# First tokens' output rows through VectorE block transpositions, a trip through DRAM and GpSimd, in place of TensorE transpositions

## The chip, the cores and the metric

The kernel runs on one core of a Trainium2 chip. The core has a matrix engine (TensorE, PE in the profile; its weight loads are PEld), three engines for elementwise work (VectorE = DVE, ScalarE = ACT, GpSimd = POOL), an engine that mostly issues transfers (SyncE = SP), and 16 DMA engines that all queues share. Each engine works through its own list of instructions in order and waits on semaphores. SBUF is the on-chip memory of 128 partitions, PSUM the accumulator memory that TensorE writes. The metric is the device time of one execution in microseconds (us).

## The reference: what is computed

One decoder layer on two groups of tokens that share the weights: 256 prompt tokens and 8 x 8 sample tokens, 320 tokens in all, with a model width of 2048. After the attention and convolution branches, the part that matters here is

```
h  = x + merged @ w_o
hn = rms_norm(h, g_ffn)
h  = h + (silu(hn @ w_gate) * (hn @ w_up)) @ w_down      # inner width 5632
y  = rms_norm(h, g_final)                                # h * rsqrt(mean(h*h) + 1e-6) * g_final
```

The final norm needs, for each token, the sum of squares over all 2048 features before any output of that token can be scaled.

## The kernel before, in words

Everything is kept with features on partitions: `hT` (its tile is called `xv` in the profile) holds 16 chunks of 128 features x 320 tokens. The weights are streamed from HBM in 512 KB pieces (`wraw`); ACT rounds each to the fast matmul format (`whi`, L129) and DVE forms the remainder (`wlo`, L130), so that three products, high by high, high by low and low by high, give the precision. TensorE runs these products back to back.

The last product, with `w_down`, is made in blocks of 512 output features (`down(half, c0)`), in two halves of the inner width (28 and 16 chunks). The last block of the second half (features 1536 to 2047, `E0` = 1536) is written out apart as the final loop (L1120 on), with its split weights held in spare tiles so that the same weights can be used twice. Each block has one `set` per pair of inner chunks (i = 0 to 6; the last set has two pairs), and its results are added to `hT` by DVE (`first`: the first 128 tokens; `rest`: the other 192).

The first 128 tokens leave in rows, a token per partition (`y0`, in tile `ya`), the other 192 with features on partitions. For the rows a part of the product (low rows of the activation by high weights, `dl`) is already made in row form and kept in `ylow`, 512 columns for each of the first three blocks; for the last block all of the correction is made in rows in the PSUM tile `rowacc`. For the first three blocks, `rows_of(c0)` transposes four 128 x 128 blocks of `hT` on TensorE against an identity matrix (L1058, PSUM tile `fa`), adds `ylow` on DVE (L1060), takes the sum of squares on ACT into one column of `ssf` (`row_squares`, L1050) and multiplies by `g_final` on DVE (L1062). `rest_of` does the squares and the scaling for the other 192 tokens; their squares are added up in `yacc`.

These steps are put off: they stand in a list, `pending`, and are taken from it at fixed places of the next block, once in the sets and once after the evictions. A context `after(...)` makes an instruction follow another in the same engine's list, without a semaphore; everything else of the order is set by a scheduler that ranks ready instructions by their place in the program and its own cost estimates. The result is one fixed list for each engine.

At the end come, on DVE, the three small instructions that sum three columns of `ssf` (`s3`, `h3`, L1138 to L1140), the evictions of the last block (L1146, L1147, L1153, L1158) with the additions to `yacc` (L1151, L1154); on TensorE eight row products (L1165), the sum of `yacc` over partitions (`pn`, L1169), the last four transpositions into `rowacc` (L1172) and the other 24 row products; then the scale factors and the stores. Tile `jk` has one buffer, `wraw` four, `whi` and `wlo` three.

Of the kernel before, what the change touches and what calls it, by code (L numbers as in the profile page):

```python
# [8 lines left out]
F32 = mybir.dt.float32  # L9
# [43 lines left out]
def hybrid_layer(ctx: ExitStack, tc: tile.TileContext, a: dict, o: list):  # L53
# [18 lines left out]
    def ps_aux(name):  # L72
        return aux[0].tile([P, 512], F32, tag="aux", name=name)
# [3 lines left out]
    def u(s):  # L77
        uid[0] += 1
        return f"{s}_{uid[0]}"
# [867 lines left out]
    def down(half, c0):  # L947

        nf, f0 = FH[half], half * FH[0]
        ps = [ps_acc(u("dn")) for _ in range(4)]  # L950
        low = ps_aux(u("dl")) if c0 < E0 else rowacc
        sets = [[k] for k in range(0, nf, 2)]
        sets[-2:] = [sets[-2] + sets[-1]]
        for i, k0s in enumerate(sets):
            parts = {}
            for k0 in k0s:
                raw = wp.tile([P, 2, 512], F32, tag="wraw", name=u("wraw"), bufs=4)
                nc.sync.dma_start(raw, w_d[c0 // 512, :, f0 + k0:f0 + k0 + 2, :])
                hi, lo = down_parts()
                split_to(hi, lo, raw)  # L960
                for j in range(2):
                    parts[k0 + j] = (hi[:, j, :], lo[:, j, :])
            end = i == len(sets) - 1
            order = [(k, c) for k in parts for c in range(4)]
            if end or i == 0:
                order.sort(key=lambda kc: kc[1])
            for k, c, m in in_turn(order, 2 if end else 4):
                cs = slice(c * P, (c + 1) * P)
                if m == 0:
                    nc.tensor.matmul(  # L970
                        turns(placed(ps[c])), parts[k][0][:, cs], turns(a_move(k)), start=k == 0, stop=False
                    )
                elif m == 1 and c == (2 if k > k0s[0] + 1 else 0):
                    nc.tensor.matmul(  # L974
                        low, a_low(k), parts[k][0], start=k == 0, stop=k == nf - 1 and c0 < E0
                    )
                elif m == 2:
                    last["mm"] = nc.tensor.matmul(  # L978
                        turns(placed(ps[c])[:, :, 0:JT]), parts[k][1][:, cs], turns(a_move(k)[:, :, 0:JT]),
                        start=False, stop=k == nf - 1,  # L980
                    )
            if len(pending) > 1 and i == 3:
                with after(last["lo"], last["mm"]):
                    pending.pop()()
        mark["out"] = []
        for c in range(4):
            k = c0 // P + c
            got, (first, rest) = placed(ps[c]), h_parts(k)
            nc.vector.tensor_add(first, first, got[:, :, 0:JR])
            nc.vector.tensor_add(rest, rest, got[:, :, JR:JT])  # L990
            mark["out"].append(nc.vector.tensor_add(rest, rest, got[:, :, JT:]))
        if c0 < E0:
            ys = ylow[:, c0:c0 + 512]
            if half == 0:
                nc.scalar.activation(ys, low, AF.Copy)
            else:
                nc.vector.tensor_add(ys, low, ys)
        if pending:
            with after(mark["out"][-1]):
                pending.pop()()  # L1000

    for half in range(2):
        f0 = 0 if half == 0 else FH[0]
# [37 lines left out]
        if half == 1:  # L1041
# [6 lines left out]
            def row_squares(i, src):  # L1048
# [2 lines left out]
                    jk[:, :src.shape[-1]], src, AF.Square, scale=D ** -0.5, accum_out=ssf[:, i:i + 1]  # L1051
                )

            def rows_of(c0):

                pt = ps_aux(u("fa"))
                for c in range(4):
                    nc.tensor.transpose(pt[:, c * P:(c + 1) * P], hT[:, c0 // P + c, 0:P], ident)  # L1058
                y = y0[:, c0:c0 + 512]
                nc.vector.tensor_add(y, pt, ylow[:, c0:c0 + 512])  # L1060
# [26 lines left out]
        for c0 in range(0, D if half == 0 else E0, 512):  # L1087
            down(half, c0)
            if half == 1:
                pending.append(lambda c0=c0: rows_of(c0))  # L1090
                pending.append(lambda c0=c0: rest_of(range(c0 // P, c0 // P + 4)))


    nf = FH[1]
# [22 lines left out]
    for i, ks in enumerate(sets):  # L1117
# [20 lines left out]
    nc.vector.tensor_reduce(s3, ssf[:, 0:3], axis=AX.X, op=ALU.add)  # L1138
    nc.vector.tensor_scalar(s3, s3, EPS, None, op0=ALU.add)
    nc.vector.tensor_scalar(h3, s3, -0.5, None, op0=ALU.mult)  # L1140
    sqs = []
    for c in range(4):
        k = E0 // P + c
# [14 lines left out]
        nc.vector.tensor_add(first, first, placed(ps[c])[:, :, 0:JR])  # L1158
    for c in range(4):
        rest_factor(E0 // P + c)  # L1160

    for k in range(nf):
        (wh, wl), xhk, xlk = held[k], a_first(k), a_low(k)
# [111 lines left out]
```

## Time and profile before

| what | value |
|---|---|
| runs of the kernel before | 1601.37, 1600.56 and 1600.24 us, median 1600.56 us |
| span of the profiled execution, first to last instruction | 1598.6 us (1.96 us less than the median; no time of its own is given for the profiled one) |
| PE busy | 1590.2 us, 99% of the span |
| PEld, DVE, ACT, POOL busy | 1554.8, 884.0, 650.6, 78.3 us |
| granted TensorE clock, mean | 0.998 |
| last load of weights issued | about 1566 us from the span's start |
| last matmul ends | about 1591 us |

Times below are counted from the span's start. A row of the timeline gives start, duration, engine, line, operation, output and inputs, and, in brackets, how long the engine had been idle and what ended it. "xN" means N like instructions merged; their duration is then that of the whole group. Matmuls overlap in the pipeline, so what one occupies is read from the start of one to the start of the next. Idle time on an engine other than TensorE costs nothing unless TensorE, or the end, waits for it.

### The profile page before, as it was taken

The page shows a single profiled execution, that of the slowest core. Times are in us where ns is not written, and L with a number is a line of the kernel's source. Part 1 is how long each engine was busy: PE and PEld are TensorE (multiplying, and loading weights), DVE is VectorE, ACT ScalarE, POOL GpSimd, SP SyncE. Part 2 cuts the span into 40 slices and gives each one's busy share as a digit, 9 for nine tenths or more (in the row PEclk, how much of TensorE's full clock was granted, in tenths as well). Part 3 has the DMA queues.
Part 4 walks back from the last instruction along what each step waited for, and adds up shares of the span by engine and source line. Part 5 has one row for each costly group of instructions (what it writes and reads, how often), then busy time and mean ns, then how long its engine had stood idle before and what let it go on. Part 6 is the DMA issues. An engine that isn't in the chain of part 4 may idle for free.

```text
span 1598.6 us, 26406 instructions
## 1 busy us (share of the span) xinstructions
PE 1590.2 (99%) x10957; PEld 1554.8 (97%) x10957; DVE 884.0 (55%) x1315; ACT 650.6 (41%) x928; POOL 78.3 (5%) x123
## 2 busy tenths in 40 slices
PE   9999999999999999999999999999999999999998
PEld 9999999999999999999999999998888999999887
DVE  7879565445555545556555555553444455555556
ACT  7555433433333334444333333333333334444443
POOL 1101311000000003320000000000000000000000
PEclk9999999999999999999999999999999999999999
DMA  7554546545444444444445454455555445545552
GB/s 271 178 169 138 185 145 195 169 156 156 157 157 158 158 158 158 156 154 155 157 159 159 158 158 156 154 155 162 156 157 158 157 158 158 158 156 154 184 180 93
DMA packets 74399, 258.13 MB, mean 161 GB/s; under 512 B 8552, under 2 KB 11928, under 8 KB 74152
## 3 DMA queue, kind: packets, MB, share of 16 engines
q1 hardware_dynamic: 71880, 249.86, 49.4%
q0 software_dynamic: 1968, 5.90, 1.3%
q8 instruction: 86, 1.41, 0.4%
q10 hardware_dynamic: 432, 0.69, 0.1%
q14 instruction: 33, 0.27, 0.0%
HBM read 253.30 MB, written 5.08 MB: 162 GB/s over the span
## 4 chain that ended last, share of the span: by engine, by line
PE 99%; DVE 0%; ACT 0%; DVEq 0%; issue 0%
PE fu L186 18%; PE fg L186 18%; PE dn L970 9%; PE ga L186 7%; PE wo L186 7%; PE gc L186 7%; PE dn L978 6%; PE B L186 3%; PE C L186 3%; PE H L186 3%; PE q L186 3%; PE ya L186 3%; PE yc L186 3%; PE dl L974 2%; PE kv L376 2%; PE dn L1125 1%
## 5 line engine op out<-in xcount | busy, mean ns | idle before, releaser
L130 DVE TENSOR_TENSOR wlo<-wraw,whi 128x1024 fp32r<-128x1024 f32 (+1 forms) x460 | 561.7, 1222 | 585.4 <-ACT whi L129 470.0
L129 ACT ACTIVATE whi<-wraw 128x1024 fp32r<-128x1024 f32 (+1 forms) x460 | 485.5, 1056 | 720.4 <-PE fu L186 129.4
L186 PE MATMUL fu<-hh_t,whi 128*128 128x320 f32 x704 | 205.1, 301 | 0.0
L186 PE MATMUL fu<-hl_t,whi 128*128 128x320 f32 x704 | 205.1, 301 | 0.0
L186 PE MATMUL fg<-hl_t,whi 128*128 128x320 f32 x704 | 205.1, 301 | 0.0
L186 PE MATMUL fg<-hh_t,whi 128*128 128x320 f32 x704 | 205.1, 301 | 0.0
L186 PE MATMUL fu<-hh_t,wlo 128*128 128x320 f32 x704 | 158.9, 301 | 0.0
L186 PE MATMUL fg<-hh_t,wlo 128*128 128x320 f32 x704 | 158.9, 301 | 0.0
L970 PE MATMUL dn<-a_t,whi 128*128 128x512 f32 x640 | 155.4, 382 | 0.0
L186 PEld LDWEIGHTS fu<-hh_t,whi 128*128 128x128 f32 x704 | 131.8, 187 | 0.0
L186 PEld LDWEIGHTS fg<-hh_t,whi 128*128 128x128 f32 x704 | 131.8, 187 | 0.0
L186 PEld LDWEIGHTS fu<-hl_t,whi 128*128 128x128 f32 x704 | 131.8, 187 | 0.0
L186 PEld LDWEIGHTS fg<-hl_t,whi 128*128 128x128 f32 x704 | 131.8, 187 | 0.0
L970 PEld LDWEIGHTS dn<-a_t,whi 128*128 128x128 f32 x640 | 115.5, 187 | 16.3 <-issue 0.9
L186 PEld LDWEIGHTS fu<-hh_t,wlo 128*128 128x128 f32 x704 | 116.2, 187 | 0.0
L186 PEld LDWEIGHTS fg<-hh_t,wlo 128*128 128x128 f32 x704 | 116.2, 187 | 0.0
L978 PEld LDWEIGHTS dn<-a_t,wlo 128*128 128x128 f32 x640 | 97.7, 188 | 6.9
L978 PE MATMUL dn<-a_t,wlo 128*128 128x320 f32 x640 | 103.4, 301 | 0.0
L186 PE MATMUL wo<-m_l,whi 128*128 128x320 f32 x256 | 74.6, 301 | 0.0
L186 PE MATMUL ga<-xl_t,whi 128*128 128x320 f32 x256 | 74.6, 301 | 0.0
L186 PE MATMUL gc<-xl_t,whi 128*128 128x320 f32 x256 | 74.6, 301 | 0.0
L186 PE MATMUL wo<-m_h,whi 128*128 128x320 f32 x256 | 74.6, 301 | 0.0
(312 smaller groups left out, 2659.0 us busy)
## 6 DMA issues: line engine op xcount, KB each, us to landing
wraw<-in_w_in_dram SPq DMA_DIRECT2D x128, 512.0 KB, 3.8
wraw<-in_w_gate_dram SPq DMA_DIRECT2D x88, 512.0 KB, 3.7
wraw<-in_w_up_dram SPq DMA_DIRECT2D x88, 512.0 KB, 3.7
wraw<-in_w_down_dram SPq DMA_DIRECT2D x88, 512.0 KB, 3.7
wraw<-in_w_o_dram SPq DMA_DIRECT2D x32, 512.0 KB, 3.8
wraw<-in_w_conv_out_dram SPq DMA_DIRECT2D x16, 512.0 KB, 3.7
wraw<-in_w_attn_out_dram SPq DMA_DIRECT2D x16, 512.0 KB, 3.6
wraw<-in_w_kv_dram SPq DMA_DIRECT2D x6, 512.0 KB, 7.5
```

Source lines behind the costliest of these rows:

```text
L129: last["hi"] = nc.scalar.activation(hi, src, AF.Copy)
L130: last["lo"] = nc.vector.tensor_sub(lo, src, hi.bitcast(F32))
L186: last["mm"] = nc.tensor.matmul(turns(fives(ps[c][:, :T])), w[:, k, c * P:(c + 1) * P], turns(x(kc)), start=(kc == 0 and i == 0), stop=(kc ...
L376: last["mm"] = nc.tensor.matmul(turns(fives(ps[c][:, :T])), w[:, k, c * P:(c + 1) * P], turns(x(kc)), start=(kc == 0 and m == 0), stop=(kc ...
L970: nc.tensor.matmul(turns(placed(ps[c])), parts[k][0][:, cs], turns(a_move(k)), start=k == 0, stop=False)
L974: nc.tensor.matmul(low, a_low(k), parts[k][0], start=k == 0, stop=k == nf - 1 and c0 < E0)
L978: last["mm"] = nc.tensor.matmul(turns(placed(ps[c])[:, :, 0:JT]), parts[k][1][:, cs], turns(a_move(k)[:, :, 0:JT]), start=False, stop=k == ...
L1125: nc.tensor.matmul(turns(placed(ps[c])[:, :, JR:]), held[k][0][:, cs], turns(a_move(k)[:, :, JR:]), start=k == 0, stop=k == nf - 1,)
```

## The change

For the first three blocks the 12 transpositions on TensorE, the three DVE additions of `ylow` and the three DVE multiplications by `g_final` are gone. In their place, for each block:

- `rows_turned(c0)`: one DVE instruction transposes 32 x 32 blocks in place of 128 x 128 (`STREAM_TRANSPOSE`, 128 x 512, into a tile with the tag `jk`); `blocks_out` then stores it to DRAM (`scr`, 256 KB) and loads it back in four pieces of 32 partitions (64 KB each), all from the GpSimd queue, which puts the 32 x 32 blocks in their places. The columns of a block stand in another order in `y0` then; `ylow` is kept in that order, `g_final` is given so and the output is put back in order outside of the measured time.
- `rows_of(c0)`: GpSimd adds `ylow` and multiplies by `g_final`; ACT takes the squares as before.

Three pieces are put on `pending` per block in place of two, and they are taken in sets 1 and 3 and after the evictions: `rows_turned`, `rest_of`, `rows_of`, first in, first out. The three small sums `s3`, `h3` are written behind the last evictions in the program.

```diff
+    def blocks_out(dst, src):
+        scr = dr.tile([P, 4, dst.shape[2]], F32, tag=f"scr{dst.shape[2]}", name=u("scr"), bufs=2)
+        nc.gpsimd.dma_start(scr, src)
+        for b in range(4):
+            nc.gpsimd.dma_start(dst[32 * b:32 * b + 32], scr[:, b].rearrange("(a i) m -> i a m", a=4))
...
-            if len(pending) > 1 and i == 3:
+            if pending and i in (1, 3):
                 with after(last["lo"], last["mm"]):
-                    pending.pop()()
+                    pending.pop(0)()
...
-            ys = ylow[:, c0:c0 + 512]
+            ys = ylow[:, c0:c0 + 512].rearrange("p (a c f) -> p c a f", a=4, c=4)
+            got = low.rearrange("p (c a f) -> p c a f", a=4, c=4)
...
+            def rows_turned(c0):
+                x = op.tile([P, 512], F32, tag="jk", name=u("jk")).rearrange("p (b m) -> p b m", b=4)
+                nc.vector.transpose(
+                    x.rearrange("p b (c f) -> p c b f", c=4),
+                    hT[:, c0 // P:c0 // P + 4, 0:P].rearrange("p c (b t) -> p c b t", b=4),
+                )
+                blocks_out(y0[:, c0:c0 + 512].rearrange("p (a m) -> p a m", a=4), x)
+
             def rows_of(c0):
-                pt = ps_aux(u("fa"))
-                for c in range(4):
-                    nc.tensor.transpose(pt[:, c * P:(c + 1) * P], hT[:, c0 // P + c, 0:P], ident)
                 y = y0[:, c0:c0 + 512]
-                nc.vector.tensor_add(y, pt, ylow[:, c0:c0 + 512])
+                nc.gpsimd.tensor_tensor(y, y, ylow[:, c0:c0 + 512], op=ALU.add)
                 row_squares(c0 // 512, y)
-                nc.vector.tensor_mul(y, y, gfb[:, c0:c0 + 512])
+                nc.gpsimd.tensor_tensor(y, y, gfb[:, c0:c0 + 512], op=ALU.mult)
...
-                pending.append(lambda c0=c0: rows_of(c0))
+                pending.append(lambda c0=c0: rows_turned(c0))
                 pending.append(lambda c0=c0: rest_of(range(c0 // P, c0 // P + 4)))
+                pending.append(lambda c0=c0: rows_of(c0))
...
-    s3, h3, v, s, r = (op.tile([P, 1], F32, name=n) for n in ("s3", "h3", "vf", "sf", "rr"))
-    nc.vector.tensor_reduce(s3, ssf[:, 0:3], axis=AX.X, op=ALU.add)
-    nc.vector.tensor_scalar(s3, s3, EPS, None, op0=ALU.add)
-    nc.vector.tensor_scalar(h3, s3, -0.5, None, op0=ALU.mult)
...                                      # the four lines stand after the last evictions
```

How the fixed lists move is seen at three places. The first is ACT at the second block's row squares (`jk,ssf<-ya`); `a_t` and `whi` are the rounded weights of the last blocks. Before:

```order
L129 ACTIVATE whi_15420<-wraw_15418 128x1024
L129 ACTIVATE a_t_12679<-wraw_15513 128x1024
L129 ACTIVATE whi_15444<-wraw_15442 128x1024
L129 ACTIVATE a_t_12679<-wraw_15517 128x1024
L129 ACTIVATE whi_15450<-wraw_15448 128x1024
```

With the change:

```order
L129 ACTIVATE whi_15431<-wraw_15429 128x1024
L1058 ACTIVATE jk_15515,ssf<-ya 128x512
L129 ACTIVATE a_t_12679<-wraw_15519 128x1024
L129 ACTIVATE whi_15455<-wraw_15453 128x1024
L129 ACTIVATE a_t_12679<-wraw_15523 128x1024
L129 ACTIVATE whi_15461<-wraw_15459 128x1024
```

The second block's squares, which need the trip through DRAM and GpSimd's addition, now stand ahead of five roundings of weights.

The second place is ACT at the end, the squares of the third block and of the last block's four chunks (`sq_15718` to `sq_15734` before, `sq_15719` to `sq_15735` after). Before:

```order
L129 ACTIVATE whi_15547<-wraw_15545 128x1024
L1050 ACTIVATE jk_15593,ssf<-ya 128x512
L1066 ACTIVATE sq_15636<-xv 128x192
L1066 ACTIVATE sq_15640<-xv 128x192
L1071 ACTIVATE xv<-xv 128x192 x2
L1066 ACTIVATE sq_15718<-xv 128x192
L1071 ACTIVATE xv<-xv 128x192
L1066 ACTIVATE sq_15723<-xv 128x192
```

With the change:

```order
L1080 ACTIVATE sq_15645<-xv 128x192
L1085 ACTIVATE xv<-xv 128x192 x2
L1080 ACTIVATE sq_15719<-xv 128x192
L1085 ACTIVATE xv<-xv 128x192
L1058 ACTIVATE jk_15682,ssf<-ya 128x512
L1080 ACTIVATE sq_15724<-xv 128x192
L1085 ACTIVATE xv<-xv 128x192
L1080 ACTIVATE sq_15730<-xv 128x192
L1085 ACTIVATE xv<-xv 128x192
L1080 ACTIVATE sq_15735<-xv 128x192
```

The third block's row squares have moved behind the first chunk's square of the last block and stand ahead of the other three.

The third place is DVE at the end (`dn_15557` to `dn_15560` are the last block's four accumulators). With the change, from the last split on:

```order
L130 TENSOR_TENSOR wlo_15554<-wraw_15551,whi_15553 128x1024
L1065 STREAM_TRANSPOSE jk_15593<-xv 128x4x4x32
L1092 TENSOR_TENSOR yacc<-yacc,sq_15633 128x192
L1092 TENSOR_TENSOR yacc<-yacc,sq_15637 128x192
L1092 TENSOR_TENSOR yacc<-yacc,sq_15641 128x192
```

and some rows further:

```order
L1158 TENSOR_TENSOR xv<-xv,dn_15558 128x192
L1162 TENSOR_TENSOR yacc<-yacc,sq_15719 128x192
L1164 TENSOR_TENSOR xv<-xv,dn_15558 128x128
L1173 TENSOR_REDUCE s_15745<-ssf 128x1
L1157 TENSOR_TENSOR xv<-xv,dn_15559 128x192
L1174 TENSOR_SCALAR s_15745<-s_15745 128x1
L1158 TENSOR_TENSOR xv<-xv,dn_15559 128x192
L1162 TENSOR_TENSOR yacc<-yacc,sq_15724 128x192
```

Before, the reduction (L1138) stood ahead of all the last block's evictions; now it stands between those of the second and the third chunk, and the third block's transposition stands behind the last split of weights. On GpSimd, which has nothing else in this stretch, each block has five transfers, then the addition, then the multiplication:

```order
L222 DMA scr_15595<-jk_15593 128x512
L224 DMA ya<-scr_15595 32x4x128 x4
L1074 TENSOR_TENSOR ya<-ya,ylow 128x512
L1076 TENSOR_TENSOR ya<-ya 128x512
L1285 UNCONDITIONAL_BRANCH
```

These rows are the third block's; nothing stands ahead of its transfers but the second block's multiplication.

More of the change, by code (lines that the diff above doesn't have):

```diff
@@ L1160, in hybrid_layer @@
         rest_factor(E0 // P + c)
+    s3, h3, v, s, r = (op.tile([P, 1], F32, name=n) for n in ("s3", "h3", "vf", "sf", "rr"))
+    nc.vector.tensor_reduce(s3, ssf[:, 0:3], axis=AX.X, op=ALU.add)
+    nc.vector.tensor_scalar(s3, s3, EPS, None, op0=ALU.add)
+    nc.vector.tensor_scalar(h3, s3, -0.5, None, op0=ALU.mult)
     for k in range(nf):
@@ L1255 @@
         inputs[n] = by_block(_np.asarray(inputs[n])[0])
+    last = E0 // 512
+    g = _np.asarray(inputs["g_final"])
+    turned = g[:E0].reshape(last, 4, 4, 32).transpose(0, 2, 1, 3)
+    inputs["g_final"] = _np.concatenate([turned.reshape(-1), g[E0:]])
     inputs["w_down"] = by_block(_np.asarray(inputs["w_down"])[0], 512)
@@ L1270 @@
     ncv = _np.asarray(res.pop()).transpose(2, 1, 0)
+    y0 = _np.asarray(res[0])
+    turned = y0[:, :E0].reshape(P, last, 4, 4, 32).transpose(0, 1, 3, 2, 4)
+    res[0] = _np.concatenate([turned.reshape(P, E0), y0[:, E0:]], axis=1)
     rest = _np.asarray(res[1]).transpose(2, 1, 0).reshape(T - P, D)
```

8 lines of the change are left out of this document (4 added, 4 removed).

## The prediction

> **What bounds the kernel now.** I read the page's busy times and its chain first, then the timeline of each engine over the last 65 us, then the transfers of the GpSimd queue.
>
> ```profile
> PE 1590.2 (99%) x10957; PEld 1554.8 (97%) x10957; DVE 884.0 (55%) x1315; ACT 650.6 (41%) x928; POOL 78.3 (5%) x123
> PE 99%; DVE 0%; ACT 0%; DVEq 0%; issue 0%
> ```
>
> TensorE is the bound from start to end: the chain that ended last is 99% PE. So an instruction taken off PE is worth what it occupies there, and work put on the other engines costs nothing until PE, or the last store, waits for it. These are the PE rows that the change touches, and the end:
>
> ```profile
> 1534.76 0.60 PE L1058 MATMUL fa<-ident,xv 128*128 128x128 f32 x4
> 1535.11 1.61 PE L970 MATMUL dn<-a_t,whi 128*128 128x512 f32 x6
> ...
> 1555.29 1.93 PE L970 MATMUL dn<-a_t,whi 128*128 128x512 f32 x8
> ...
> 1561.96 0.60 PE L1058 MATMUL fa<-ident,xv 128*128 128x128 f32 x4
> 1562.32 1.26 PE L1125 MATMUL dn<-a_t 128*128 128x384 f32 x6
> ...
> 1567.40 0.60 PE L1058 MATMUL fa<-ident,xv 128*128 128x128 f32 x4
> 1567.75 1.58 PE L1125 MATMUL dn<-a_t 128*128 128x384 f32 x8
> ...
> 1582.69 2.03 PE L1165 MATMUL rowacc<-a_t 128*128 128x512 f32 x8
> 1584.56 0.51 PE L1169 MATMUL pn<-yacc,ones_r 128*128 128x192 f32 x2
> ```
>
> Each group of transpositions occupies 0.35, 0.36 and 0.35 us from its start to the next. The last two rows are the only place where PE needs something late from DVE: `pn` reads `yacc`. DVE there:
>
> ```profile
> 1536.83 0.35 DVE L991 TENSOR_TENSOR xv<-xv,dn 128x192 f32<-128x192 f32 x1
> ...
> 1564.30 0.69 DVE L1060 TENSOR_TENSOR ya<-fa,ylow 128x512 f32<-128x512 f32 x1
> 1564.90 1.22 DVE L130 TENSOR_TENSOR more<-wraw,more 128x1024 fp32r<-128x1024 f32 x1
> ...
> 1573.04 0.68 DVE L1060 TENSOR_TENSOR ya<-fa,ylow 128x512 f32<-128x512 f32 x1
> ...
> 1575.46 0.15 DVE L1138 TENSOR_REDUCE s<-ssf 128x1 f32<-128x3 f32 x1
> 1575.64 0.36 DVE L1078 TENSOR_TENSOR yacc<-yacc,sq 128x192 f32<-128x192 f32 x1
> ...
> 1581.66 0.35 DVE L1146 TENSOR_TENSOR xv<-xv,dn 128x192 f32<-128x192 f32 x1
> ...
> 1584.06 0.36 DVE L1154 TENSOR_TENSOR yacc<-yacc,sq 128x192 f32<-128x192 f32 x1
> ```
>
> The third chunk's evictions start at 1581.66 and the last addition to `yacc` ends at 1584.42, 0.14 us before `pn`. PE does not wait there now, but there is no slack: what delays DVE at 1581.66 delays PE by nearly as much.
>
> **The sum: gain.** PE loses 0.35 + 0.36 + 0.35 = 1.06 us of work. By the end all PE times stand 1.06 us earlier, so the third chunk's evictions are due at 1581.66 - 1.06 = 1580.60.
>
> **First two blocks.** ACT has the second block's row squares ahead of five roundings; the rows of before there, and of the third block's squares:
>
> ```profile
> 1544.35 1.06 ACT L129 ACTIVATE whi<-wraw 128x1024 fp32r<-128x1024 f32 x1 [1.08 <-PE dl L974]
> 1547.81 1.06 ACT L129 ACTIVATE a_t<-wraw 128x1024 fp32r<-128x1024 f32 x1 [2.40 <-DMA wraw<-in_w_down_dram]
> 1548.77 1.05 ACT L129 ACTIVATE whi<-wraw 128x1024 fp32r<-128x1024 f32 x1
> ...
> 1570.81 1.06 ACT L129 ACTIVATE whi<-wraw 128x1024 fp32r<-128x1024 f32 x1 [1.53 <-DMA wraw<-in_w_down_dram]
> 1573.82 0.63 ACT L1050 ACTIVATE jk<-ya 128x512 f32<-128x512 f32 x1 [1.95 <-DVE ya L1060]
> 1574.36 0.19 ACT L1050 ACTIVATION_READ_ACCUMULATOR jk<-ya 128x1 f32 x1
> ```
>
> The `whi` of 1548.77 feeds the PE set at 1555.29. One `a_t` rounding (0.96 to the next start) and its own 1.06 stand ahead of that set, so ACT may be held until 1553.2. The second transposition stands behind the eviction of 1536.83, at 1537.1: its chain may take 16.1 us. Below I put the chain at 11.0 us in a quiet machine and 16.1 at worst, so I cost this at nothing; ACT's lead over PE is the cover, and beyond it PE would wait for what is over. I take the first block the same way, its chain being the same. `rest_of` stays in set 3 of the next block. The evictions of `ylow` with four-dimensional shapes I take at their old price, DVE having idle time ahead of them.
>
> **Third block.** Its transposition stands on DVE behind the last split, where the addition of `ylow` stood at 1573.04. One removed addition (0.60, from 1564.30 to 1564.90) frees the buffer of the last load that much earlier; the `whi` of 1570.81 waits for that load, so 0.60 comes off, and 0.71 of earlier PE: it starts at 1573.04 - 0.60 - 0.71 = 1571.73. From there everything is one chain: transposition, store, four loads, GpSimd's addition, ACT's square, DVE's reduction. The rows nearest to its links:
>
> ```profile
> out_dram<-ya SPq DMA_DIRECT2D x2, 256.0 KB, 2.8
> out_dram<-vn POOLq DMA_DIRECT2D x1, 128.0 KB, 4.0
> bias_s<-e_scr POOLq DMA_DIRECT2D x1, 68.0 KB, 2.9
> e_scr<-e_sb POOLq DMA_DIRECT2D x1, 24.0 KB, 2.2
> cv<-in_cache_v_dram POOLq DMA_DIRECT2D x8, 128.0 KB, 5.0
> ...
> 40.31 0.52 POOL L459 DMA_DIRECT2D e_scr<-e_sb  x1 [23.21 <-PE prb L211]
> 42.76 0.54 POOL L460 DMA_DIRECT2D bias_s<-e_scr  x1 [1.43 <-DMA e_scr<-e_sb]
> ...
> 608.53 0.72 POOL L909 TENSOR_TENSOR sq<-xv 128x320 f32<-128x320 f32 x1 [0.87 <-DVE xv L899]
> 622.10 1.70 POOL L909 TENSOR_TENSOR sq<-xv 128x320 f32<-128x320 f32 x1
> ...
> 1574.00:1582.00 8.00, 8.00 (x54) 8.00 (x53) 4.39 (x15) 3.35 (x10) 0.00 (x0) 1.00 0.00 0
> ```
>
> The last row (its last two figures are the DMA share and GB/s) says that the DMA engines are idle from 1574 to 1582, so I take prices near the quiet rows:
>
> - Transposition: no row shows one. I take the DVE row of equal size, 0.69; as upper end 1.22, the row of twice as many elements.
> - Store of 256 KB from GpSimd's queue: between 2.2 (24 KB, same queue) and 4.0 (128 KB, same queue, beside weight loads). SP's 256 KB store at a quiet end takes 2.8; I take 3.1.
> - Four loads of 64 KB: three issues of 0.54 ahead of the last, 1.62, and its landing. The nearest row is 68 KB, 2.9, which I take: 4.5. Ends: 2.2 and 5.0, so 3.8 and 6.6.
> - GpSimd's addition: 0.72 for 320 columns, times 512/320, 1.15. The same operation took 1.70 where DVE worked beside it; upper end 2.72.
> - ACT's square with its read of the sum: 1573.82 to 1574.55, 0.73.
> - Hand-overs: from landing to the dependent GpSimd issue 42.76 - 40.31 - 2.2 = 0.25, twice; three between engines at 0.10 (1573.72 to 1573.82): 0.8.
>
> Sum: 0.69 + 3.1 + 4.5 + 1.15 + 0.73 + 0.8 = 10.97 (11.0). By the low ends 0.69 + 2.2 + 3.8 + 1.15 + 0.73 + 0.8 = 9.4, by the high ends 1.22 + 4.0 + 6.6 + 2.72 + 0.73 + 0.8 = 16.1. The reduction can start at 1571.73 + 10.97 = 1582.70 and takes 0.18 to the next start (1575.46 to 1575.64). The evictions behind it, due at 1580.60, start at 1582.88: 2.28 late. The two other small sums, which now stand between dependent evictions, add about 0.1. ACT's remaining squares, queued behind the row squares, come in time for evictions so late. So PE waits 2.4 us ahead of `pn`, and everything behind it (24 row products, scales, stores) follows.
>
> The Trainium skill, "DMA: Bandwidth & Descriptors", section "Anatomy of one DMA — SWDGE (gpsimd) path", states some 2.0 us plus bytes/436e3 for such a transfer. My estimate from it is 2.6 for the store and 2.15 for a load, 1.25 us less in the sum, and the end would be unchanged within 0.1 us instead of 1.3 later, within the band of the forecast below. The row of 128 KB at 4.0 speaks against it under load, that of 24 KB at 2.2 for it.
>
> A second rule there speaks against the change: "GPSIMD Engine Reference", section "Engine selection", gives two-input elementwise work to VectorE, GpSimd being about twice as slow, and the page's key points name contention with VectorE instructions of two SBUF inputs. The trace agrees (0.72 against 1.70 above). By the page's factor alone the addition would take 1.4, the sum 0.2 more.
>
> **Sum.** -1.06 + 2.4 = +1.3 us: the span of 1598.6 becomes 1599.9. The runs' median lies 1.96 above the span, so 1601.9 us. That is inside 0.2% (3.2 us), about what a measurement of this kernel can tell from no change.
>
> **Rivals.**
>
> *The chain is hidden* (15 in 100). If the chain takes under 8.7 us (1580.60 - 0.18 - 1571.73), only the small sums in DVE's list remain: 0.18 + 0.1. Then -1.06 + 0.3 = -0.8, 1599.8 us. For it: idle DMA engines and the row of 2.2. Against it: even the low ends give 9.4.
>
> *The trip through DRAM runs at its loaded prices* (30 in 100), the slower side. One mechanism: a GpSimd transfer takes 4 to 5 us whatever else runs, as in the rows of 4.0 and 5.0. At 4.0 and 6.6, with the rest as above, the chain is 14.0 and the wait 5.4: +4.3, 1604.9 us. With the other high ends too, 16.1, it is 1607.0. The rise is past 0.2% from a chain of 12.9 us on. For it: most GpSimd rows of before are so long. Against it: all those were taken beside weight loads, and the window of 1574 is empty.
>
> *The second block starves PE* (3 in 100): a chain above 16.1 us at 1537.1 holds ACT beyond 1553.2. One us over is one us of PE, on top of the third block's wait; some 1608. Only the far ends together reach it.
>
> The forecast has 50 in 100, for waits from 0.7 to 4.2 us; 2 in 100 are left for a gain above 3.2 us, for which no row gives a place.
>
> **How the numbers follow.** Low end 1599.6: the hidden chain, 0.2 lower for the spread of runs. High end 1606.0: the loaded prices with about half of their spread. Outside lie some 5 in 100 below and 13 above. Faster by over 0.2% 0.03; slower 0.32, from the loaded prices and the starved second block; the same 0.65.
>
> **What would show it.** No `fa` rows on PE and three starts 0.35 earlier. A gap on PE ahead of `pn` of some 2.4 us, ended by DVE's `yacc`; on DVE an idle time ahead of the reduction, ended by ACT's `jk`; on ACT, `jk` waiting for GpSimd's `ya` with idle time in front. The store's and loads' times to landing decide between the rivals. No idle time on PE in the blocks at 1528 to 1562. The prediction would be wrong if a block transposition takes many times 0.69, if GpSimd's transfers land slower than 5 us in a quiet machine, or if GpSimd's work slows DVE's evictions at the end.

## The result, and the profile after

| what | before | after |
|---|---|---|
| median of the runs, us | 1600.51 (1599.53 to 1601.37, and one of 4330.16) | 1602.87 (1601.82 to 1604.79) |
| ratio, with its 95% interval | | 1.0016 (1.0010 to 1.0022) |
| profiled execution: time, span, us | span 1598.6 | 1604.61, span 1602.9 |
| PE busy, us | 1590.2 | 1591.4 |

The changed kernel is 0.16% (2.4 us) slower: inside the band of 0.2% (its interval reaches just beyond it), and 1.0 us above the time forecast. The profiled execution is one of the slower ones of the changed kernel. The other executions lie in two groups, about two thirds of them from 1601.8 to 1603.5 and the rest from 1604.0 to 1604.8; why there are two is part of what follows.

The busy times and the chain on the page of the kernel after:

```profile
PE 1591.4 (99%) x10945; PEld 1554.9 (97%) x10945; DVE 882.5 (55%) x1312; ACT 650.0 (41%) x928; POOL 94.5 (6%) x144
PE 98%; DVE 1%; DMA 1%; ACT 0%; POOL 0%; issue 0%; DVEq 0%; ACTq 0%
```

PE has 12 matmuls fewer and yet 1.2 us more of busy time. Its timeline, from a place ahead of the change to its end:

```profile
1496.88 0.62 PE L981 MATMUL dl<-whi,a_t 128*128 128x512 f32 x2
...
1535.31 1.58 PE L977 MATMUL dn<-a_t,whi 128*128 128x512 f32 x6
...
1582.12 2.01 PE L1180 MATMUL rowacc<-a_t 128*128 128x512 f32 x8
1585.98 0.59 PE L1184 MATMUL pn<-yacc,ones_r 128*128 128x192 f32 x2 [1.85 <-DVE yacc L1165]
1586.41 0.60 PE L1187 MATMUL rowacc<-ident,xv 128*128 128x128 f32 x4
1586.76 1.66 PE L1180 MATMUL rowacc<-a_t 128*128 128x512 f32 x4
1588.22 3.12 PE L1180 MATMUL rowacc<-more,a_t 128*128 128x512 f32 x8
1591.18 2.92 PE L1180 MATMUL rowacc<-whi,a_t 128*128 128x512 f32 x12
```

The first row stands at 1496.33 in the trace of before, so this execution is 0.55 us late before anything has changed; in the other traces of this document the same row stands between 1495.84 and 1496.78, whatever the kernel, so such offsets are taken off before two traces are compared. The transpositions `fa` are gone from PE. Ahead of `pn` PE now waits for `yacc`, 1.85 us. And eight row products that took 2.0 us take 3.12. The windows over that stretch say why (PEclk is the third figure from the end):

```profile
1584.00:1586.00 2.00, 0.15 (x2) 0.02 (x1) 1.92 (x8) 1.22 (x3) 0.07 (x1) 1.00 0.00 0
1586.00:1588.00 2.00, 2.00 (x10) 1.75 (x11) 0.94 (x1) 0.75 (x3) 0.00 (x0) 0.81 0.03 8
1588.00:1590.00 2.00, 2.00 (x6) 1.54 (x6) 1.79 (x5) 0.00 (x0) 0.00 (x0) 0.50 0.00 0
1590.00:1592.00 2.00, 2.00 (x9) 1.66 (x8) 2.00 (x5) 0.00 (x0) 0.00 (x0) 0.84 0.34 132
```

Behind the wait the granted clock falls to 0.50 and is back after 3.4 us (1587.2 to 1590.6, worked out from the clocks of the three windows). The last matmul ends at 1594.10. In the trace of before the last row of PE is this:

```profile
1588.11 2.92 PE L1165 MATMUL rowacc<-whi,a_t 128*128 128x512 f32 x12
```

From the start of `pn` to the end of the last matmul it is 1594.10 - 1585.98 = 8.12 us after, 1591.03 - 1584.56 = 6.47 before: 1.65 us more, 1.5 of them from the fall (an execution without a fall, the next run, takes 6.62).

The chain of the third block, on the timelines of DVE, POOL and ACT (and one of the last evictions):

```profile
1573.11 0.70 DVE L1065 STREAM_TRANSPOSE jk<-xv 128x512 f32<-128x512 f32 x1
...
1582.73 0.16 DVE L1173 TENSOR_REDUCE s<-ssf 128x1 f32<-128x3 f32 x1 [1.74 <-ACT jk L1058]
...
1583.45 0.83 DVE L1162 TENSOR_TENSOR yacc<-yacc,sq 128x192 f32<-128x192 f32 x1
```

```profile
1538.64 0.60 POOL L222 DMA_DIRECT2D scr<-jk  x1 [10.69 <-DVE jk L1065]
1543.54 2.18 POOL L224 DMA_DIRECT2D ya<-scr  x4 [4.29 <-DMA scr<-jk]
1549.95 1.28 POOL L1074 TENSOR_TENSOR ya<-ya,ylow 128x512 f32<-128x512 f32 x1 [4.23 <-DMA ya<-scr]
...
1574.11 0.60 POOL L222 DMA_DIRECT2D scr<-jk  x1 [20.76 <-DVE yacc L1092]
1576.70 2.18 POOL L224 DMA_DIRECT2D ya<-scr  x4 [1.99 <-DMA scr<-jk]
1580.53 1.41 POOL L1074 TENSOR_TENSOR ya<-ya,ylow 128x512 f32<-128x512 f32 x1 [1.65 <-DMA ya<-scr]
1582.77 1.30 POOL L1076 TENSOR_TENSOR ya<-ya 128x512 f32<-128x512 f32 x1 [0.84 <-ACT jk L1058]
```

```profile
1551.26 0.63 ACT L1058 ACTIVATE jk<-ya 128x512 f32<-128x512 f32 x1 [5.70 <-POOL ya L1074]
...
1552.84 1.05 ACT L129 ACTIVATE whi<-wraw 128x1024 fp32r<-128x1024 f32 x1
...
1554.73 1.05 ACT L129 ACTIVATE whi<-wraw 128x1024 fp32r<-128x1024 f32 x1
...
1570.87 1.06 ACT L129 ACTIVATE whi<-wraw 128x1024 fp32r<-128x1024 f32 x1 [1.62 <-DMA wraw<-in_w_down_dram]
...
1581.97 0.63 ACT L1058 ACTIVATE jk<-ya 128x512 f32<-128x512 f32 x1 [1.82 <-POOL ya L1074]
```

From the transposition to the reduction it is 1582.73 - 1573.11 = 9.62 us in the third block. In the second block, with weight loads on the same DMA engines, the trip takes far longer: from the store's issue to the first load's it is 4.90 us (1538.64 to 1543.54) where the third block has 2.59, and behind the loads' issues POOL is idle for 4.23 us where it has 1.65.

The last stores take nearly as long as before (2.9, 3.0 and 1.8 us to landing against 2.8, 2.8 and 1.9, medians of one to two stores), but the stretch from the last matmul to the end of the span has grown from 1598.6 - 1591.03 = 7.6 to 1602.9 - 1594.10 = 8.8 us. The waits of SyncE's queue over that stretch, after and then before, show part of it (us in all, times, longest; L1285 and L1266 are the program's end):

```profile
SPq L1285 <- DMA out_dram<-ya: 2.8, 2, 2.0
...
SPq L1285 <- PEq L1285: 1.1, 2, 0.9
```

```profile
SPq L1266 <- DMA out_dram<-ya: 2.6, 2, 1.8
SPq L1266 <- PEq L1266: 0.7, 2, 0.5
```

So for the profiled execution: 0.55 of offset, -1.06 of transpositions, 0.1 in the second block, 1.85 of wait, 1.65 behind the wait and 1.2 at the end make 4.3 us, which is the difference of the spans, 1602.9 - 1598.6.

### The profile page after: what moved, and what is told of

It is laid out like the page before. It is cut to its first block, busy times and chain, and to the rows that moved or that the text cites. A ratio compares the mean times of both kernels' runs of the same rounds, so it can differ in the third digit from the quotient of the medians.

```text
span 1602.9 us, 26432 instructions
## 1 busy us (share of the span) xinstructions
PE 1591.4 (99%) x10945; PEld 1554.9 (97%) x10945; DVE 882.5 (55%) x1312; ACT 650.0 (41%) x928; POOL 94.5 (6%) x144
## 3 DMA queue, kind: packets, MB, share of 16 engines
q8 instruction: 86, 1.41, 0.3%
## 4 chain that ended last, share of the span: by engine, by line
PE 98%; DVE 1%; DMA 1%; ACT 0%; POOL 0%; issue 0%; DVEq 0%; ACTq 0%
PE fu L186 18%; PE fg L186 18%; PE dn L977 9%; PE wo L186 7%; PE gc L186 7%; PE ga L186 7%; PE dn L985 6%; PE B L186 3%; PE C L186 3%; PE H L186 3%; PE q L186 3%; PE ya L186 3%; PE yc L186 3%; PE dl L981 2%; PE kv L383 2%; PE rowacc L1180 0%
## 5 line engine op out<-in xcount | busy, mean ns | idle before, releaser
L186 PE MATMUL gc<-xh_t,whi 128*128 128x320 f32 x256 | 74.5, 301 | 0.0
L186 PE MATMUL ga<-xh_t,whi 128*128 128x320 f32 x256 | 74.5, 301 | 0.0
```

The source lines that it names most:

```text
L186: last["mm"] = nc.tensor.matmul(turns(fives(ps[c][:, :T])), w[:, k, c * P:(c + 1) * P], turns(x(kc)), start=(kc == 0 and i == 0), stop=(kc ...
```

## The experiments

Each kernel below was timed beside runs of the kernel before; differences are against the medians of those (1600.38 to 1600.72). By my estimate a median of such a run is good to some 0.2 to 0.3 us; the interval given with it is wider, some 1.4 us to either side, and no difference below reaches 2%.

### The change again

> The changed kernel once more, nothing edited. Theory A (the wait): PE waits 1.8 to 2.0 us ahead of pn, less 1.06 us of removed transpositions, and loses up to 1.6 us more where the granted clock falls after that wait; the wait is in every execution, the fall not, so the times lie in two groups near 1602.4 and 1604.4 us, median 1602.5. Rival B (many small costs): the same median, one group only.

Measured: 1603.02 us, ratio 1.0018 (1.0009 to 1.0027). The profiled execution has a span of 1601.0, a wait at `pn` of 1.41 us, no fall of the clock, and a wait of 0.37 us in the second block:

```profile
1555.86 1.59 PE L977 MATMUL dn<-a_t,whi 128*128 128x512 f32 x6 [0.37 <-ACT whi L129]
...
1585.55 0.59 PE L1184 MATMUL pn<-yacc,ones_r 128*128 128x192 f32 x2 [1.41 <-DVE yacc L1165]
...
1589.21 2.96 PE L1180 MATMUL rowacc<-whi,a_t 128*128 128x512 f32 x12
```

What follows: the two groups are executions without and with the fall of the clock. Those above 1603.9 us, here and in the change's first runs, have a mean granted clock of 0.997, all others 0.998 or 0.999. This execution, near the median's distance from before (1601.0 - 1598.6 = 2.4), has none; from the start of `pn` to the end of the last matmul it takes 1592.17 - 1585.55 = 6.62 us. Its PE ends at 1592.17, 1.14 late, and 1.2 us come behind it. Of the 1.14, the second block has 0.65: the same `dl` matmul is 0.40 ahead of before at 1550 and 0.25 behind it at 1561.

### The third block's squares late

```diff
-                nc.scalar.activation(sq, hT[:, k, P:T], AF.Square)
+                last["sq"] = nc.scalar.activation(sq, hT[:, k, P:T], AF.Square)
...
-    nc.vector.tensor_add(yacc, yacc, sqs[3])
+    last["sum"] = nc.vector.tensor_add(yacc, yacc, sqs[3])
+    with after(last["sq"]):
+        rows_scaled(E0 - 512)
...
+    with after(last["sum"]):
+        nc.vector.tensor_reduce(s3, ssf[:, 0:3], axis=AX.X, op=ALU.add)
```

`rows_scaled` holds the row squares and GpSimd's multiplication; the two sums behind the reduction move with it.

> The third block's row squares stand on ACT behind the squares of the last block's four chunks, the three small sums on DVE behind the last addition to yacc; all else is the changed kernel. Theory A: no wait ahead of pn (under 0.4 us), no fall of the clock, 1.06 us gained: 1599.5 us (1599.2 to 1600.2), and one group of times. Rival B (first two blocks, GpSimd beside DVE, the traffic): little of the loss goes, 1602 us or more.

Measured: 1600.92 us, ratio 1.0003 (0.9995 to 1.0012): 2.1 us faster than the change, so the third block's place in ACT's and DVE's lists is most of the loss. It is 1.4 us above what was expected. In its profile PE waits twice:

```profile
1556.10 1.59 PE L977 MATMUL dn<-a_t,whi 128*128 128x512 f32 x6 [0.52 <-ACT whi L129]
...
1585.01 0.59 PE L1193 MATMUL pn<-yacc,ones_r 128*128 128x192 f32 x2 [0.61 <-DVE yacc L1171]
```

The first wait is in the second block, which loses 0.87 us in all there (`dl` at 1550 and at 1561, as above). The second comes of one instruction on DVE beside one on POOL:

```profile
1580.71 1.49 DVE L1168 TENSOR_TENSOR yacc<-yacc,sq 128x192 f32<-128x192 f32 x1
...
1582.97 0.35 DVE L1168 TENSOR_TENSOR yacc<-yacc,sq 128x192 f32<-128x192 f32 x1
```

```profile
1580.70 1.29 POOL L1074 TENSOR_TENSOR ya<-ya,ylow 128x512 f32<-128x512 f32 x1 [1.61 <-DMA ya<-scr]
```

### The same without GpSimd's addition

```diff
-                nc.gpsimd.tensor_tensor(y, y, ylow[:, c0:c0 + 512], op=ALU.add)
+                if c0 + 512 < E0:
+                    nc.gpsimd.tensor_tensor(y, y, ylow[:, c0:c0 + 512], op=ALU.add)
```

> The run with the third block's row squares late, and GpSimd's addition of ylow left out for the third block (512 of the columns of the first 128 tokens lack that term). Theory (GpSimd's addition of two SBUF tiles stops VectorE's addition of two SBUF tiles: yacc took 1.49 us beside it and 0.35 elsewhere): all four yacc additions of the last block take 0.35 to 0.40, and TensorE's wait ahead of pn, 0.61 us, is gone or below 0.1; 1600.92 - 0.6 = 1600.3. Rival (the 1.49 us have another cause, such as a wait that the profile puts into the instruction): yacc stays above 1 us and the wait stays.

Measured: 1600.77 us, ratio 1.0001 (0.9992 to 1.0010). All four additions take 0.35 to 0.36 us, and the wait at `pn` is gone:

```profile
1580.42 0.35 DVE L1169 TENSOR_TENSOR yacc<-yacc,sq 128x192 f32<-128x192 f32 x1
...
1583.46 0.36 DVE L1172 TENSOR_TENSOR yacc<-yacc,sq 128x192 f32<-128x192 f32 x1
```

So it is GpSimd's addition of two SBUF tiles that holds up VectorE's addition of two SBUF tiles, for all of its 1.29 us. Instructions with one input in PSUM are not held up: in the changed kernel the addition of `xv` and `dn` at 1580.71, beside the same GpSimd instruction, takes its usual 0.28. The median moved by 0.15 us alone, not by 0.6, and each of the two medians is 0.4 us above its own runs of before. The profiled execution of the run before this one was the slowest of its runs, so what the collision costs in the median is not shown to be more than that.

### The third block as before

```diff
+                if c0 + 512 == E0:
+                    return rows_before(c0)
```

`rows_before` is `rows_of` of the kernel before. The three small sums stand where they were, too.

> The third block's rows are made as before (TensorE, DVE), the small sums stand as before; the first two blocks go by DRAM and GpSimd as changed. Theory A: two of three groups of transpositions gained, 0.71 us, no wait ahead of pn: 1599.8 us (1599.5 to 1600.4). Rival B, the first two blocks' holding of ACT by 7 us each costs: 1601.5 us or more.

Measured: 1600.94 us, ratio 1.0004 (0.9995 to 1.0013). There is no wait at `pn`, which starts at 1584.56, but one in the second block, which loses 0.53 us there in all:

```profile
1556.03 1.60 PE L977 MATMUL dn<-a_t,whi 128*128 128x512 f32 x6 [0.22 <-ACT whi L129]
```

The time lies between the 1599.8 of theory A and the 1601.5 of the rival. With 0.7 us of work taken off PE the kernel is still 0.5 us above before: something other than the third block costs about 1.2 us.

### The first blocks' squares put behind the roundings

```diff
-            with after(mark["out"][-1]):
+            with after(mark["out"][-1], last["hi"]):
                 pending.pop(0)()
```

> Only the first two blocks changed, the third as before, and the row squares of a block stand on ScalarE behind that block's last rounding of weights. Theory: the wait ahead of the second block's last set (0.22 us in the run without the pin) goes, 0.7 us of transpositions is saved, and nothing else is touched: 1600.94 - 0.2 to 0.5, so 1600.4 to 1600.7, and the wait on TensorE's dn is gone from the profile. Rival (the first blocks cost something else, such as GpSimd's work beside VectorE, or a later end): no less than 1600.9, with the wait gone.

Measured: 1600.95 us, ratio 1.0003 (0.9994 to 1.0012). The wait in the second block is gone, and the `dl` matmuls there keep their distance to before from 1550 to 1561. The time did not move, as the rival has it: what the second block loses is seen in the traces (0.53 us in the run above, 0.02 here) and not in the medians. The rest of the loss must lie behind PE:

```profile
1587.72 2.94 PE L1196 MATMUL rowacc<-whi,a_t 128*128 128x512 f32 x12
```

PE ends at 1590.66, 0.4 earlier than in before, but the span at 1599.2, 8.5 us behind it and not 7.6.

### Before, with a delay of VectorE ahead of pn

```diff
     nc.vector.tensor_add(yacc, yacc, sqs[3])
+    for _ in range(5):
+        nc.vector.tensor_scalar(yacc, yacc, 1.0, None, op0=ALU.mult)
```

> The kernel before, with yacc multiplied by 1.0 five times on DVE behind its last addition, so that pn comes about 1.95 us later and TensorE idles so long; nothing else differs. If a wait there costs only its length: 1602.4 us. Theory A with the clock: in some or all executions the granted clock is halved for some 3 us behind the wait, 1.5 us more: 1602.4 to 1604.0 us, and a row of windows with a clock near 0.5 behind pn.

Measured: 1601.72 us, ratio 1.0008 (0.9999 to 1.0017). The scheduler moved `pn` behind other row products, so PE did not wait, and the time came out below what was expected. The loss of 1.25 came by another way: `pn` is also the first step of DVE's scale factors and of the 3.77 us of scaling behind them, and that chain then ends later than PE.

The same with `pn` held at its place by `after`, with five and with nine such steps:

> The kernel before with five idle steps on VectorE behind the last addition to yacc (5 x 0.39 = 1.95 us) and pn held at its place, so that TensorE must wait some 1.8 us there as in the changed kernel. Theory: 1600.5 + 1.8 = 1602.3 without a fall of the clock, 1603.8 in executions in which the clock falls to 0.50 behind the wait; a time between, with two groups about 1.5 us apart. Rival (only the late chain behind pn counts, TensorE's wait does not): as with the same delay and no wait, 1601.7.

> The same with nine steps: 3.5 us of delay, a wait of some 3.4 us. Theory: the clock falls in most or all executions: 1600.5 + 3.4 + 1.5 = 1605.4; without a fall 1603.9. If the clock's fall needs no wait of a certain length but comes by chance, its share is as with five steps.

Measured: 1601.91 us, ratio 1.0009 (1.0000 to 1.0018), with five steps, and 1604.31 us, ratio 1.0021 (1.0012 to 1.0030), with nine. A step cost less than I took, 0.29 us (five took 1.44, nine 2.62), so the waits were 1.22 and 2.41 us. The `pn` row and the window behind it, of the shorter delay and then of the longer:

```profile
1586.36 0.59 PE L1172 MATMUL pn<-yacc,ones_r 128*128 128x192 f32 x2 [1.22 <-DVE yacc L1156]
```

```profile
1588.00:1590.00 2.00, 2.00 (x10) 1.62 (x9) 1.83 (x4) 0.00 (x0) 0.00 (x0) 1.00 0.00 0
```

```profile
1586.81 0.59 PE L1172 MATMUL pn<-yacc,ones_r 128*128 128x192 f32 x2 [2.41 <-DVE yacc L1156]
```

```profile
1588.00:1590.00 2.00, 2.00 (x7) 1.52 (x6) 1.86 (x3) 0.17 (x1) 0.00 (x0) 0.50 0.00 0
```

With a wait of 1.22 us the time rises by 1.45, the clock stays at 1.00 and all executions lie within 1.2 us. With 2.41 us it rises by 3.85, and the executions lie in two groups again, 1602.6 to 1603.2 and 1604.2 to 1604.9, the larger part in the upper one. So the later `pn` is paid in full. With five steps that is not yet the wait of PE: the same delay without a wait cost 1.25. And the longer wait brings, in part of the executions, a halved clock, 1.5 us more; that the lower group is the executions without a fall is taken from the two groups, since none of them has a trace and their mean clock, 0.998, is also found in the upper one.

Narrower windows put the fall at 1587.5 to 1590.9 here and at 1587.2 to 1590.6 in the changed kernel: 3.41 us both times. In all fourteen traces the clock stays at 1.00, or at 0.50, for whole multiples of 3.413 us (1580.4 us, 463 times, then 3.41 at 0.50, then 6.83 in the changed kernel), with edges that lie elsewhere from trace to trace. In the four traces with a wait of more than 1 us at `pn`, the wait lies whole within one such stretch: 1.85 of 3.41 us and 2.41 of 3.41 were followed by a stretch at 0.50, 1.22 and 1.41 were not. That executions whose edges cut the wait in two escape the fall would explain the two groups; no run here tests it.

Nothing of the change is in these kernels, so the fall needs neither GpSimd's work nor the trip through DRAM.

### The changed kernel with pn later

```diff
-        if k == 3:
+        if k == 7:
```

> The changed kernel with the sum over partitions (pn) and the last four transpositions behind 16 of the 32 row products in place of 8, so that TensorE has 2.0 us more work ahead of them. Theory (TensorE's wait ahead of pn, and the clock that falls behind it, are the loss): no wait at pn, no clock below 0.95 in the row products; the end is then set by the scale factors and stores behind pn, which come as late as in the changed kernel or a little later, as in the run of before with five delays (1601.72): 1601.0 to 1601.9. Rival (the loss is the late chain of scales and stores behind pn and has nothing to do with TensorE's wait): no gain against the changed kernel, 1602.5 to 1603.5.

Measured: 1602.63 us, ratio 1.0013 (1.0004 to 1.0022). PE waits nowhere and its clock never falls; it ends at 1590.11, 0.9 before its end in the kernel before. And the gain over the change is 0.2 to 0.4 us: my theory here was wrong and the rival right. `pn` starts at 1585.35, and DVE comes last:

```profile
1589.08 3.77 DVE L1197 TENSOR_TENSOR wraw<-xv,rnr 128x576 f32<-128x576 f32 x7
1592.76 0.15 DVE L1202 SCALAR_TENSOR_TENSOR vf<-ssf,h 128x1 f32<-128x1 f32 x1
```

From `pn` to that step it is 7.41 us here and 7.32 before (1591.88 - 1584.56), where ACT's last square was ready 0.13 us ahead of it:

```profile
1591.56 0.19 ACT L1050 ACTIVATION_READ_ACCUMULATOR jk<-rowacc 128x1 f32 x1
...
1591.88 0.16 DVE L1187 SCALAR_TENSOR_TENSOR vf<-ssf,h 128x1 f32<-128x1 f32 x1
```

The two ways to the end, over PE and over DVE's scaling, were equal within 0.2 us in the kernel before, and `pn` stands at the head of both. A later `pn` is a later end, whether PE waits or not.

### What lengthens the end

Every kernel with the change has 0.9 to 1.3 us more behind PE than before (the one above apart, where DVE comes last). Two kernels put parts of it into the kernel before: the transposition on VectorE and the trip through DRAM of the first two blocks, with the result written over; or ten small memsets of GpSimd in their place.

```diff
+            if i == 1 and trips:
+                with after(last["lo"], last["mm"]):
+                    trips.pop()()
```

> The kernel before, with the block transposition and the trip through DRAM (one store, four loads on GpSimd's queue) of the first two blocks added; what is loaded is then written over, as before, by VectorE's addition, so TensorE's work and ScalarE's list are those of before. In all runs with the change so far the end of the span comes 0.9 to 1.0 us later behind pn than in the runs without it, also where only the first two blocks are changed and TensorE waits for nothing. Theory (the late transfers on GpSimd's queue lengthen the last stores and the last waits of SyncE and GpSimd): 1600.5 + 0.9 = 1601.4, with the last matmul where it was and SyncE's last DRAIN starting 0.3 us or more behind the landing of the last store (0.07 in before). Rival (the rows of y0, made in another way, do it): no change, 1600.5.

> The kernel before, with ten small memsets of GpSimd (on columns that are then written over) at the places where the trips of the first two blocks stood, and no transfer. Theory of the late transfers: no change, 1600.5. Rival (longer instruction lists on GpSimd, whose code is then fetched near the end): later by the same 0.9 as with the trips, 1601.4.

Measured: 1600.64 us, ratio 1.0001 (0.9992 to 1.0010), with the trips, and 1600.47 us, ratio 1.0000 (0.9991 to 1.0009), with the memsets. Both are too near to before to be told from it by time, and the 0.9 us that the theory gave the trips did not come; the profile tells more. With the trips the end is 1598.5 - 1590.56 = 7.9 us behind PE, 0.4 longer. SyncE's list closes with three instructions called DRAIN; the first of them (not the last, as my expectation has it) is the long one that the changed kernel has too, and starts 0.3 us later behind the last wait. The group's shortest, median and longest duration in ns come first, then its first and last start. With the memsets all three take 7 ns. The rows of before, of the changed kernel and of the trips alone:

```profile
L1266 SPq DRAIN  x3: 7/7/7, 1597.8 to 1598.1; - x3
```

```profile
L1285 SPq DRAIN  x3: 7/7/130, 1601.5 to 1601.9; - x3
```

```profile
L1284 SPq DRAIN  x3: 7/7/129, 1597.6 to 1598.0; - x3
```

The trips cause it, but not necessarily as transfers: with them SyncE's list is longer by four waits. The last run makes SyncE's list longer far ahead of the end, by 39 tiny loads, so that its end stands elsewhere in it:

```diff
                 nc.sync.dma_start(raw, w_d[c0 // 512, :, f0 + k0:f0 + k0 + 2, :])
+                if half == 0 and c0 < E0 and k0 < 26:
+                    n = (c0 // 512 * 13 + k0 // 2)
+                    nc.sync.dma_start(pad[:, n:n + 1], a["g_final"][0:1].rearrange("(p n) -> p n", p=1))
```

> The pinned kernel (first two blocks changed), with 39 four-byte loads on SyncE's queue far ahead, in the first half of w_down, so that SyncE's list is longer there and its last instructions stand elsewhere in the list; the lists of the other engines are the same. In every run with trips SyncE has 980 recorded instructions instead of 976, its last DRAIN starts 0.36 to 0.38 us behind its last wait (0.07 without trips) and takes 0.12 to 0.13 (0.007). Theory (SyncE stalls where its instructions cross into a part of its code that has to be fetched, and the four extra waits move that place into the end): the DRAIN starts 0.07 behind the last wait and takes 0.01, so the end comes 0.4 us earlier, 1600.95 - 0.4 = 1600.5; if the third store, whose issue took 0.89 instead of 0.33, stalled for the same reason, 1600.0. Rival (transfers on GpSimd's queue lengthen the DRAIN by themselves): unchanged, 1600.95.

Measured: 1600.43 us, ratio 0.9999 (0.9990 to 1.0008), 0.3 us below before, where the same kernel without the shift was 0.5 above. DRAIN is short again, and the end 8.0 us behind PE instead of 8.5 (rows of the run with the shift):

```profile
L1308 SPq DRAIN  x3: 7/7/7, 1597.5 to 1597.8; - x3
```

```profile
q14 instruction: 1, 0.01, 0.1%
```

The second row (count, MB, share) is from the transfers of 1545 to 1562: a fetch of instructions, 8 KB, that now stands there. In the pinned run the same window has none, and one starts at 1598.88, 0.66 us behind the start of the long DRAIN. Such a fetch stands 0.63 to 0.67 us behind it in each of the eight traces with a long DRAIN, and in none of the others. So 0.4 to 0.5 us of the end is set by where SyncE's last instructions stand in its list, and not by the trips as such. That this place is a crossing into the next piece of code is argued from the fetches; the fetch comes too late to be what the DRAIN waited for, and the profile does not say whose it is. The Trainium skill, "Runtime: NRT & Kernel Launch", section "Instruction fetch mechanics", says that a sequencer fetches its own code in blocks of 16 KiB and that crossing one is mostly hidden. The trace has such fetches, 86 of 16 KB on queue 8 and 36 of 8 KB (0.29 MB) on queue 14; if the place is a crossing, this one was not hidden, since it fell behind the last store. The third store's long issue, on the other hand, stayed (0.77 us for 0.33), so the theory is borne out for the DRAIN alone. In the three traces with a long issue another fetch on queue 14 starts about 0.1 us ahead of it, and in none of the others; what it does there was not tested.

## Why the prediction was right, and where it was not

**The bound and the gain** held. PE is 98% of the chain that ended last, and the rows behind the first block stand 0.35 to 0.40 us earlier relative to a place ahead of the change, for 0.35 forecast.

**The first two blocks** were costed at nothing, and that was wrong. ACT's square came at 1551.26, inside my limit of 1553.2, and PE still lost time: 0.11 us in the profile after, 0.65 in the second run of the change, and from 0.03 to 0.87 in the four other traces with this order on ACT. The limit was wrong: the last set of a block needs both last pieces of weights within its first matmuls (in the second run PE stops behind the second one), so the `whi` at 1554.73, the second behind that of 1552.84, had to be ready near 1555.7. And the chain took 14.4 us (from its transposition at 1537.64 to the end of ACT's read at 1551.99), not the 11.0 of a quiet machine. So the rival that starves PE needed no chain above 16.1 us; its 3 in 100 were worked out from the wrong limit. Put behind the roundings, the squares cost PE nothing (0.02 us).

**The third block's chain** was 9.62 us for 10.97 forecast, nearest to the low ends: 2.59 from the store's issue to the loads' for 3.35, 3.83 from there to the addition for 4.75 (hand-overs included), the addition 1.41 for 1.15. The block transposition took 0.70 for 0.69. The lower estimate that the prediction gave beside its sum, 1.25 us less, was the nearer one. The transposition started later than I put it, 1573.11 less the offset of 0.55 against 1571.73, because the `whi` of 1570.87 still waited for its load. That load was issued 0.91 us earlier than before, but took 4.98 us for 4.59 to land, so of the 1.31 us forecast (0.60 and 0.71) only 0.49 came. The two errors cancel in part, which is luck: the reduction at 1582.73 less 0.55 is 1582.18, for 1582.70.

**The wait at `pn`** is there, ended by `yacc`, as the prediction said: 1.41 and 1.85 us for 2.4. The rival with loaded prices fell: the third block's transfers landed in the quiet times. Its prices are about right for the first two blocks (4.90 and 6.41 us there, from issue to issue and from issue to the addition, for 4.0 and 6.6).

**The sum** of +1.3 lacked three terms. The first is the second block's loss, above. The second is the fall of the clock behind the wait, 1.5 us in about a third of the executions. The third is the stretch behind PE, for which I had no change at all and which grew by 1.2 us: some 0.4 of it is the place of SyncE's last instructions, as the last run shows; the rest, 0.1 us in DVE's last steps, 0.3 of a later landing and 0.5 at GpSimd's last instructions, was not taken apart, and its cause stays open. With the terms as measured in an execution without a fall (-1.06 of transpositions, 0.65, 1.41, 0.15 behind `pn`, 1.2 at the end) the sum is 2.35, the 2.4 of that execution's span. The median of all executions rose by 2.36; of those without a fall it is 1602.53, a rise of 2.0, since the second block's loss differs from one to the next. So the mechanism at `pn` was forecast, and that the time came within 1.0 us is in part luck: a wait put 0.6 to 1.0 us too long stood against about 2 us of terms at nothing.

**What I had named as breaking the forecast**, GpSimd slowing DVE's evictions at the end, did happen in a small way, though to the additions of squares and not to the evictions themselves: an addition to `yacc` of 0.83 us beside GpSimd's multiplication in the changed kernel, and of 1.49 beside its addition in the run with late squares. The Trainium skill, "GPSIMD Engine Reference", section "Key points", names this contention for VectorE instructions with two SBUF inputs; the trace agrees, 1.49 and 0.83 us against 0.35.

## What to carry to other kernels

An operation whose result heads two chains of equal length, here the sum over partitions, ahead of both the last matmuls and the scaling, is priced by its start, not by the wait that one engine shows: taking the wait off TensorE gave 0.2 to 0.4 us back of 2.4. A saving of 1 us in 1600 is smaller than what the end of the program can move by itself, so the stretch from the last matmul to the last instruction has to be compared first. And work that is put off must be placed behind the work that the bound engine needs next, on every queue that it passes.

## What the runs showed of the hardware

- The granted TensorE clock fell to 0.50 for 3.41 us behind a single wait of 1.85 us, and of 2.41 us, and not behind 1.22 or 1.41 us (one trace each); by the two groups of times, it did not fall in all executions of the kernels with the longer waits. The Trainium skill, "TensorE: Matmul & The Clock Gate", section "HAM oscillation — how this bites in real kernels", gives gaps over some 3.4 us as the rule; these were shorter. The Trainium skill, the same page, Part 1, section "What's actually happening", has the clock set by a window of 3413 ns that runs freely; the traces agree, with changes of the clock 3.413 us or whole multiples of it apart and edges that are not tied to the program, and that would fit that only part of the executions show the fall.
- A GpSimd addition of 128 x 512 in SBUF (1.29 us) stopped a VectorE addition of two SBUF tiles for its whole length (1.49 for 0.35 us), and an addition with one PSUM input beside such a GpSimd addition not at all (0.28 us).
- A trip through DRAM from GpSimd's queue took 2.6 us from the 256 KB store's issue to the loads' with no other transfers under way, and 4.9 beside the weight loads.
- Thirty-nine transfers of four bytes, far from the end, shortened the end by 0.5 us: the DRAIN behind SyncE's last wait took 7 ns in place of 116, and came 0.3 us sooner. With them an 8 KB fetch of instructions moved away from the end.
